# A two-layer decoder on one core: sums of weights formed in the landing buffers, four of these, halved splits of the sums, and a cross output projection with both feature tiles in one bank

## The chip, the core and the metric

The kernel runs on one core of a Trainium2 chip. The metric is the device time of one execution in microseconds (us); lower is better. All inputs and the output lie in device memory; nothing is computed on the host. The engines are TensorE (PE, with its weight load PEld), VectorE (DVE), ScalarE (ACT), GpSimd (POOL) and SyncE (SP), which issues the loads of the weights.

## The reference

Two layers, each of three parts, on 256 tokens of width 2048, all in float32:

```python
for l in range(DEPTH):                                   # DEPTH = 2
    h = rms_norm(x, attn_norm[l])
    (mq, mk, mv, dq, dk, dv, sq, sk, sv, iq, ik, iw) = _split_columns(h @ w_in[l])
    # three kinds of heads: MoBA (6), differential (4), sparse by an index (6)
    mixed = jnp.concatenate([o_moba, o_diff, o_dsa], axis=-1)
    x = x + mixed @ w_out[l]

    h = rms_norm(x, cross_norm[l]); m = rms_norm(mem, mem_norm[l])
    # 4 heads of attention over 256 memory tokens, giving co (256 x 512)
    x = x + co @ cross_wo[l]

    h = rms_norm(x, ffn_norm[l])
    u = h @ ffn_w_up[l]                                  # 2048 -> 2 x 5504
    # a causal convolution over 3 tokens gives uc; g, val = the halves of uc
    x = x + (jax.nn.silu(g) * val) @ ffn_w_down[l]       # 5504 -> 2048
```

The query and key gains of the three kinds of heads (`moba_qk_gain`, `diff_qk_gain`, `dsa_qk_gain`) and the convolution's weights are given per layer.

## The kernel before

**Products in two parts.** Each float32 operand is split in a rounded part `hi` and a rest `lo`, and a product is the sum of two or three matmuls of the parts. Weights are loaded by SP into a landing tile `raw` (8 KB in each partition, three buffers, `RAWS`). `halves` (line 79 on ACT, line 81 on DVE) makes `hi` as a copy of `raw` and then `lo` as `raw` minus `hi`; both tiles have three buffers (`HIS`). A `raw` tile is free again after its `lo`, a `hi` and a `lo` tile after the last matmul that reads them. Activations are split in the same way: `parts` (lines 266 and 267) makes the two tiles `a`.

**Stages of a layer.** The input projection and the three kinds of attention, the output projection with its residual, cross attention with its output projection, the up projection with convolution and gate (21 steps of two tiles and a last one), and the down projection. Tiles of `k`, `t` and `a` are slots of 512 floats in pools that rotate. `mm_rows` (lines 220 to 222) holds the tokens on the output's rows, `up_acc` (lines 242 to 246) the features; there, a pair of 128 features takes two PSUM banks (`mm`, four of them), and a group of weights is 8 blocks of 128 rows.

**Side work.** Everything that isn't a weight stream is written as generators, which a heap runs by a counter of ticks: each group of matmuls calls `tick`, and a generator that yields d goes on d ticks later. `factors` (line 410) yields `G_R`, then sums squares over features by matmuls with ones (line 416), from a tile to which POOL adds one pair after the other (line 408), and makes the root-mean-square factor `rx`. A tile framework then fixes each engine's order of instructions by its own estimate of when operands are ready; so the order on an engine is not that of the code.

**The residual.** `residual` calls `up_acc` for eight pairs of feature tiles, adds them to the residual `xT` and starts `take`, which splits the new `xT` for the next stage. For the cross output projection (`whole=True`) each pair ends with two adds of 256 columns on DVE (line 437), one for each bank.

**The down projection.** `down` runs once for each of two column halves of 1024, over 22 steps: 21 pairs of 128-row blocks of weights and one single block. Seven of the pairs (`SEVEN`) multiply a 2 x 2 block form by the scheme with seven products, the others by eight. The seven-product steps need sums of the activations (`s4`, lines 298 to 301) and of the weights (`tt`, lines 303 to 305, DVE, into a tile `sum` with one buffer), and then two pairs of `hi` and `lo`: one of 3 x 512 columns from `raw`, one of 4 x 512 from `sum`:

```python
tt = wp.tile([P, 4, CH], F32, tag="sum", name="sum", bufs=1)
...
w = halves(b[:, 1:4, :], 3, CH)
sx = parts(s, 4 * P)
wt = halves(tt, 4, CH)
```

Such a step loads its weights with three DMAs (lines 292 to 294), an ordinary one with one (line 318). After the 22 steps `combine` reads eight banks (the four `mm` and four of `at`) with DVE adds and, in the last layer, stores the result (line 1064).

## Time and profile before

| | |
|---|---|
| median of 3 runs | 2567.83 us (2561.11 to 2570.95) |
| the profiled execution's own time | 2556.22 us |
| its span in the profile | 2554.4 us |
| mean granted clock of TensorE | 0.997 |
| PE busy | 2514.4 us, 98% |
| DVE busy | 1910.2 us, 75% |
| ACT busy | 1364.4 us, 53% |
| POOL busy | 162.8 us, 6% |
| moved by DMA | 459.89 MB, mean 180 GB/s |

Busy times are sums over an engine's instructions in one profiled execution. The ends of pipelined matmuls are modelled, so PE's share says little by itself; what tells is where PE stands idle, and for whom. In a row of the waits, the first name is what waited, the one behind the arrow what ended the wait, then come the microseconds, the number of waits and the longest. In a row of the windows come the window, its length, and each engine's busy time with its instructions, the granted clock of TensorE, the DMA engines' busy share and the GB/s.

### The profile page before, as it was taken

To read this page: it belongs to the slowest core of one execution; us is meant where nothing else is said; L and a number is where in the kernel's file an instruction comes from. 1 tells how busy PE (TensorE), PEld (TensorE's weight loads), DVE (VectorE), ACT (ScalarE), POOL (GpSimd) and SP (SyncE) were. 2 spreads that over 40 slices of the span, in tenths; PEclk is the share of its full clock that TensorE was granted. 3 is DMA by queue.
4 is the path that set the end of the run, shared out by engine and by line. 5 is a ranking of instruction groups with operands and counts; after the bars stand their busy time and mean duration, and the time that the engine had idled before them with its cause. 6 is when DMAs were issued, how large, how long until landed. Compare 5 with 4: busy or idle time off the path is not lost. (4 is left out here: it accounts for less than half of the span.)

```text
span 2554.4 us, 34687 instructions
## 1 busy us (share of the span) xinstructions
PE 2514.4 (98%) x13402; PEld 2146.4 (84%) x13402; DVE 1910.2 (75%) x2982; ACT 1364.4 (53%) x1756; POOL 162.8 (6%) x177
## 2 busy tenths in 40 slices
PE   8999999999999999999999999999999999999999
PEld 7778888888888888877787788888888888888777
DVE  6876766677777777889968767666777777778888
ACT  5555565455554555556545555554555555555554
POOL 2210101010000000000041011010100000000000
PEclk9999999999999999999999999999999999999999
DMA  7545546555566656555654555564556665664554
GB/s 240 165 151 177 167 153 201 166 168 189 183 197 186 193 188 192 173 198 173 215 162 146 164 170 164 161 213 133 185 186 193 188 192 184 196 189 163 192 195 152
DMA packets 377705, 459.89 MB, mean 180 GB/s; under 512 B 10638, under 2 KB 331076, under 8 KB 377540
## 3 DMA queue, kind: packets, MB, share of 16 engines
q1 hardware_dynamic: 377540, 457.67, 55.8%
q8 instruction: 105, 1.72, 0.3%
q14 instruction: 60, 0.49, 0.1%
HBM read 455.54 MB, written 2.10 MB: 179 GB/s over the span
## 5 line engine op out<-in xcount | busy, mean ns | idle before, releaser
L81 DVE TENSOR_TENSOR lo<-raw,hi 128x2048 fp32r<-128x2048 f32 (+4 forms) x466 | 969.7, 2084 | 356.0 <-ACT hi L79 354.7
L245 PE MATMUL mm<-k,hi 128*128 128x512 f32 x3136 | 1098.4, 393 | 3.2 <-DVE xT L437 3.2
L79 ACT ACTIVATE hi<-raw 128x2048 fp32r<-128x2048 f32 (+4 forms) x466 | 811.2, 1744 | 434.5 <-PE mm L221 164.0
L246 PE MATMUL mm<-k,lo 128*128 128x256 f32 x3264 | 914.4, 280 | 0.1
L245 PEld LDWEIGHTS mm<-k,hi 128*128 128x128 f32 x3136 | 586.8, 187 | 133.2 <-issue 3.5
L246 PEld LDWEIGHTS mm<-k,lo 128*128 128x128 f32 x3264 | 617.1, 189 | 0.8 <-DVE lo L81 0.5
L220 PE MATMUL mm<-hi,k 128*128 128x512 f32 (+2 forms) x1088 | 413.8, 380 | 0.0
L221 PE MATMUL mm<-hi,k 128*128 128x512 f32 (+2 forms) x1088 | 404.3, 372 | 0.0
L222 PE MATMUL mm<-lo,k 128*128 128x512 f32 (+2 forms) x1088 | 401.6, 370 | 1.0 <-DVE lo L81 1.0
L220 PEld LDWEIGHTS mm<-hi,k 128*128 128x128 f32 x1088 | 206.3, 190 | 35.8 <-issue 3.3
L222 PEld LDWEIGHTS mm<-lo,k 128*128 128x128 f32 x1088 | 205.5, 189 | 36.1 <-DVE lo L81 1.8
L221 PEld LDWEIGHTS mm<-hi,k 128*128 128x128 f32 x1088 | 206.3, 190 | 32.6 <-issue 2.6
L285 PE MATMUL mm<-lo,a 128*128 128x512 f32 x548 | 216.4, 395 | 15.7 <-DVE lo L81 15.7
L283 PE MATMUL mm<-hi,a 128*128 128x512 f32 x548 | 214.6, 392 | 0.2 <-DVE t L1027 0.2
L284 PE MATMUL mm<-hi,a 128*128 128x512 f32 x548 | 214.4, 391 | 0.0
L1040 ACT ACTIVATE t<-t 128x256 f32<-128x256 f32 x86 | 35.7, 418 | 229.3 <-DVE t L1032 229.3
L285 PEld LDWEIGHTS mm<-lo,a 128*128 128x128 f32 x548 | 103.5, 189 | 43.2 <-DVE lo L81 21.9
L1027 DVE TENSOR_TENSOR t<-mm,t 128x256 f32<-128x256 f32 x172 | 68.8, 421 | 90.3 <-ACT t L1024 90.3
L1024 ACT ACTIVATE t<-mm 128x256 f32<-128x256 f32 x172 | 60.2, 375 | 142.2 <-PE mm L246 142.2
L408 POOL TENSOR_TENSOR k<-k,t 128x512 f32<-128x512 f32 x35 | 52.2, 1492 | 1138.0 <-ACT t L407 976.1
L283 PEld LDWEIGHTS mm<-hi,a 128*128 128x128 f32 x548 | 103.7, 189 | 21.6 <-issue 0.6
L284 PEld LDWEIGHTS mm<-hi,a 128*128 128x128 f32 x548 | 103.6, 189 | 21.8
(242 smaller groups left out, 2571.7 us busy)
## 6 DMA issues: line engine op xcount, KB each, us to landing
raw<-in_ffn_w_up_dram SPq DMA_DIRECT2D x168, 1024.0 KB, 5.1
raw<-in_w_in_dram SPq DMA_DIRECT2D x152, 512.0 KB, 4.5
raw<-in_ffn_w_down_dram SPq DMA_DIRECT2D x56, 1024.0 KB, 5.6
raw<-in_w_in_dram SPq DMA_DIRECT2D x20, 1024.0 KB, 5.0
raw<-in_w_out_dram SPq DMA_DIRECT2D x16, 1024.0 KB, 5.5
raw<-in_cross_wkv_dram SPq DMA_DIRECT2D x16, 1024.0 KB, 5.0
raw<-in_ffn_w_down_dram SPq DMA_DIRECT2D x32, 512.0 KB, 5.2
raw<-in_ffn_w_down_dram SPq DMA_DIRECT2D x56, 256.0 KB, 3.8
```

The lines of the kernel that those rows point to most:

```text
L79: nc.scalar.activation(hi, src, AF.Copy)
L81: nc.vector.tensor_tensor(lo, src, hi.bitcast(F32), OP.subtract)
L220: nc.tensor.matmul(o, lhsT=xh, rhs=hi[:, j, :], start=first, stop=False)
L221: nc.tensor.matmul(o, lhsT=xl, rhs=hi[:, j, :], start=False, stop=False)
L222: ins = nc.tensor.matmul(o, lhsT=xh, rhs=lo[:, j, :], start=False, stop=last)
L245: nc.tensor.matmul(outs[i], lhsT=wh, rhs=acts[k], start=first, stop=False)
L246: ins = nc.tensor.matmul(outs[i][:, :S], lhsT=wl, rhs=acts[k][:, :S], start=False, stop=last)
L283: nc.tensor.matmul(bank[q], lhsT=x[0], rhs=w[0], start=first, stop=False)
L284: nc.tensor.matmul(bank[q], lhsT=x[1], rhs=w[0], start=False, stop=False)
L285: return nc.tensor.matmul(bank[q], lhsT=x[0], rhs=w[1], start=False, stop=left[q] == 0)
L1024: nc.scalar.activation(uv[:, S:], outs[i][:, S:], AF.Copy)
L1027: nc.vector.tensor_tensor(u, outs[i][:, :S], v, OP.add)
```

## The change

Six things are changed together.

- Landing buffers `raw` and `hi` buffers go from three to four; `lo` buffers are counted by themselves (`LOS`, three). The tile `sum` is gone, `tmp` has seven buffers and not eight, and the convolution's weights of both layers share one tile.
- In a seven-product step the sums of weights are formed in the landing tile itself, by four adds of 512 columns (line 310 after the change), and these stand behind the step's own `lo`, since they overwrite what it reads.
- `hi` and `lo` of the sums are made in two halves: blocks 0 and 3, then 1 and 2.
- `factors` waits five ticks, or three where it has more to do behind it (in the cross output projection), instead of three.
- In the cross output projection both feature tiles of a pair lie in the halves of one bank, and one add of 512 columns takes them.
- The head gains come per layer, in slots, with three small loads for each layer; in layer 1 these stand between the two groups of index weights.

```diff
@@ -29,9 +29,9 @@
 NEG = -1.0e30
 GONE = -3.0e38
 TOPK = 64
-G_R, G_T, G_S, G_PT, G_DN = 3, 5, 1, 3, 3
+G_R, G_T, G_S, G_PT, G_DN = 5, 5, 1, 3, 3
 FIRST_COL = 3328
-KP, AP, RAWS, HIS = 38, 8, 3, 3
+KP, AP, RAWS, HIS, LOS = 38, 8, 4, 4, 3
 SEVEN = frozenset((2, 5, 8, 11, 14, 16, 18))
 GW = 2 * CH
 
@@ -62,7 +62,7 @@
         return kp.tile([P, CH], F32R, tag="a", name="a", bufs=AP)
 
     def tmp():
-        return tp.tile([P, CH], F32, tag="t", name="t", bufs=8)
+        return tp.tile([P, CH], F32, tag="t", name="t", bufs=7)
 
     def pmm():
         return ps.tile([P, CH], F32, tag="mm", name="mm")
@@ -73,12 +73,14 @@
     def new_raw(a, n):
         return wp.tile([P, a, n], F32, tag="raw", name="raw", bufs=RAWS)
 
-    def halves(src, a, n):
+    def halves(src, a, n, steps=(slice(None),)):
 
         hi = wp.tile([P, a, n], F32R, tag="hi", name="hi", bufs=HIS)
-        nc.scalar.activation(hi, src, AF.Copy)
-        lo = wp.tile([P, a, n], F32R, tag="lo", name="lo", bufs=HIS)
-        nc.vector.tensor_tensor(lo, src, hi.bitcast(F32), OP.subtract)
+        lo = wp.tile([P, a, n], F32R, tag="lo", name="lo", bufs=LOS)
+        for v in steps:
+            nc.scalar.activation(hi[:, v, :], src[:, v, :], AF.Copy)
+        for v in steps:
+            nc.vector.tensor_tensor(lo[:, v, :], src[:, v, :], hi[:, v, :].bitcast(F32), OP.subtract)
         return hi, lo
 
 
@@ -126,8 +128,9 @@
     def attn_g(l):
         return gA[:, l * KT:(l + 1) * KT]
 
+    cw = cst.tile([P, 4, 2 * NF], F32, name="cw")
+
     def load_conv(l):
-        cw = cst.tile([P, 4, 2 * NF], F32, name=f"cw{l}")
         cv = slot()[:2 * NF, :].rearrange("f (j p) -> f j p", p=P)
         nc.sync.dma_start(cv[:, 0:3, :], ffn_conv_w[l].rearrange("j (f p) -> f j p", p=P))
         nc.sync.dma_start(cv[:, 3, :], ffn_conv_b[l].rearrange("(f p) -> f p", p=P))
@@ -140,7 +143,6 @@
             nc.vector.tensor_copy(cw.rearrange("p j f -> p (j f)"), pt[:, :8 * NF])
 
         step(rest())
-        return cw
 
 
 
@@ -228,7 +230,9 @@
     def up_acc(wview, runs, acts, order=None, whole=False):
 
 
-        outs = [pmm() for _ in range(2)]
+
+        outs = [pmm() for _ in range(1 if whole else 2)]
+        own = [outs[0][:, i * S:(i + 1) * S] if whole else outs[i][:, :S] for i in range(2)]
         order = order or EIGHTS
         first = True
         for gi, grp in enumerate(order):
@@ -239,12 +243,12 @@
                 for i in range(2):
                     wh, wl = hi[:, j, i * P:(i + 1) * P], lo[:, j, i * P:(i + 1) * P]
                     if whole:
-                        nc.tensor.matmul(outs[i][:, :S], lhsT=wh, rhs=acts[k][:, :S], start=first, stop=False)
-                        nc.tensor.matmul(outs[i][:, :S], lhsT=wh, rhs=acts[k][:, S:], start=False, stop=False)
+                        nc.tensor.matmul(own[i], lhsT=wh, rhs=acts[k][:, :S], start=first and i == 0, stop=False)
+                        nc.tensor.matmul(own[i], lhsT=wh, rhs=acts[k][:, S:], start=False, stop=False)
                     else:
                         nc.tensor.matmul(outs[i], lhsT=wh, rhs=acts[k], start=first, stop=False)
-                    ins = nc.tensor.matmul(outs[i][:, :S], lhsT=wl, rhs=acts[k][:, :S], start=False,
-                                           stop=last)
+                    ins = nc.tensor.matmul(own[i], lhsT=wl, rhs=acts[k][:, :S], start=False,
+                                           stop=last and (i == 1 or not whole))
                 first = False
                 if j % 4 == 3 or j == n - 1:
                     tick(ins)
@@ -299,18 +303,16 @@
                                         OP.subtract)
                 nc.vector.tensor_tensor(s4[:, 2, :], s4[:, 1, :], a4[:, 0, :], OP.add)
                 nc.vector.tensor_tensor(s4[:, 3, :], a4[:, 2, :], s4[:, 2, :], OP.subtract)
-                tt = wp.tile([P, 4, CH], F32, tag="sum", name="sum", bufs=1)
-                nc.vector.tensor_tensor(tt[:, 0:2, :], b[:, 1::2, :], b[:, 0:1, :].to_broadcast([P, 2, CH]), OP.add)
-                nc.vector.tensor_tensor(tt[:, 2, :], tt[:, 1, :], b[:, 1, :], OP.add)
-                nc.vector.tensor_tensor(tt[:, 3, :], tt[:, 2, :], b[:, 2, :], OP.add)
                 a = parts(act[i], 4 * P)
                 w = halves(b[:, 1:4, :], 3, CH)
                 sx = parts(s, 4 * P)
-                wt = halves(tt, 4, CH)
+                for o, x, y in ((3, 0, 3), (0, 0, 1), (1, 3, 1), (2, 1, 2)):
+                    nc.vector.tensor_tensor(b[:, o, :], b[:, x, :], b[:, y, :], OP.add)
+                wt = halves(b, 4, CH, (slice(0, 4, 3), slice(1, 3)))
                 A, Sx = (lambda j, v=v: [u[:, j * P:(j + 1) * P] for u in v] for v in (a, sx))
                 B, T = (lambda j, v=v: [u[:, j, :] for u in v] for v in (w, wt))
-                todo = {1: (A(0), B(0)), 2: (A(2), B(1)), 3: (Sx(3), B(2)), 4: (A(3), T(3)), 5: (Sx(1), T(0)),
-                        6: (Sx(2), T(2)), 7: (Sx(0), T(1))}
+                todo = {1: (A(0), B(0)), 2: (A(2), B(1)), 3: (Sx(3), B(2)), 4: (A(3), T(2)), 5: (Sx(1), T(0)),
+                        6: (Sx(2), T(1)), 7: (Sx(0), T(3))}
                 for q in (1, 2, 3, 5, 7, 6, 4):
                     ins = product(q, *todo[q])
             else:
@@ -409,7 +411,7 @@
 
     def factors(acc, rest=None):
 
-        yield G_R
+        yield G_R if rest is None else G_R - 2
         pt = pat()
         for t in range(NT):
             for j in range(2):
@@ -432,9 +434,7 @@
             outs = up_acc(wview, [(2 * i * P, 2 * P)], acts, order[i], whole)
             pair = xT[:, 2 * i:2 * i + 2, :].rearrange("p k s -> p (k s)")
             if whole:
-                for j in range(2):
-                    v = xT[:, 2 * i + j, :]
-                    nc.vector.tensor_tensor(v, outs[j][:, :S], v, OP.add)
+                nc.vector.tensor_tensor(pair, outs[0], pair, OP.add)
             else:
                 u = tmp()
                 for j in range(2):
@@ -508,12 +508,19 @@
         nc.gpsimd.tensor_copy(ropeI[:, 1, :, 0, 32:], s)
 
     TAB_W = {"d": 64, "s": 128, "m": 128}
-    head_gain = {}
-    for kind, g in (("d", diff_qk_gain), ("s", dsa_qk_gain), ("m", moba_qk_gain)):
-        gb = cst.tile([P, L, 2, TAB_W[kind]], F32, name="gb" + kind)
-        nc.sync.dma_start(gb.rearrange("p l a d -> p (l a d)"),
-                          g.rearrange("l a d -> (l a d)").unsqueeze(0).to_broadcast([P, L * 2 * TAB_W[kind]]))
-        head_gain[kind] = gb
+    def head_gains(l):
+
+        res, row = {}, None
+        for kind, g in (("d", diff_qk_gain), ("s", dsa_qk_gain), ("m", moba_qk_gain)):
+            n = 2 * TAB_W[kind]
+            if row is None or kind == "m":
+                row, o = slot(), 0
+            nc.sync.dma_start(row[:, o:o + n], g[l].rearrange("a d -> (a d)").unsqueeze(0).to_broadcast([P, n]))
+            res[kind] = row[:, o:o + n].rearrange("p (a d) -> p a d", a=2)
+            o += n
+        return res
+
+    head_gain = head_gains(0)
     lam = slot()
     nc.sync.dma_start(lam, diff_lambda.rearrange("l a d -> (l a d)").unsqueeze(0).to_broadcast([P, L * 256]))
     nlams = cst.tile([P, L], F32, name="nlams")
@@ -533,7 +540,7 @@
 
         w = TAB_W[kind]
         st, h = 128 // w, w // 2
-        gb = head_gain[kind][:, l]
+        gb = head_gain[kind]
         tb = [slot()[:, :NT * 2 * w].rearrange("p (t a d) -> p t a d", t=NT, a=2) for _ in range(2)]
         for a in range(2):
             g1 = gb[:, a, :h].unsqueeze(1).to_broadcast([P, NT, h])
@@ -842,6 +849,8 @@
                 rotary()
                 rope_index()
                 lambdas()
+        if l:
+            head_gain.update(head_gains(l))
         for k in "dsm":
             tabs[k] = rope_table(l, k)
         ib = mm_rows(hT, wv, [(6144 + half, half)], QUADS)
@@ -1009,7 +1018,7 @@
 
         residual(coT, cwo, [[range(2), range(2, 4)]] + [[range(4)]] * 7, gB[:, (2 * L + l) * KT:(2 * L + l + 1) * KT], h3, spread, whole=True)
 
-        cw = load_conv(l)
+        load_conv(l)
 
 
         up = ffn_w_up[l].rearrange("(k p) n -> p k n", p=P)
```

The program's order on three engines, before and after. On DVE in the down projection of layer 1, up to the third seven-product step; before (`lo<-sum` is the rest of a step's sums, `lo<-raw` of 2048 columns that of an ordinary step and of 1536 that of a seven-product step, `a` the rest of activations, lines 303 to 305 the sums of weights):

```order
L81 TENSOR_TENSOR lo<-sum,hi 128x2048
L267 TENSOR_TENSOR a<-k,a 128x512
L303 TENSOR_TENSOR sum<-raw 128x1024
L304 TENSOR_TENSOR sum<-sum,raw 128x512
L81 TENSOR_TENSOR lo<-raw,hi 128x2048
L267 TENSOR_TENSOR a<-k,a 128x512
L81 TENSOR_TENSOR lo<-raw,hi 128x2048
L305 TENSOR_TENSOR sum<-sum,raw 128x512
L267 TENSOR_TENSOR a<-k,a 128x512
L81 TENSOR_TENSOR lo<-raw,hi 128x1536
L267 TENSOR_TENSOR a<-t,a 128x512
```

After (line 83 is the old line 81, 271 the old 267, 304 and 305 the old 300 and 301, and line 310 the sums):

```order
L83 TENSOR_TENSOR lo<-raw,hi 128x2048
L271 TENSOR_TENSOR a<-k,a 128x512
L83 TENSOR_TENSOR lo<-raw,hi 128x2048
L271 TENSOR_TENSOR a<-k,a 128x512
L83 TENSOR_TENSOR lo<-raw,hi 128x1536
L271 TENSOR_TENSOR a<-t,a 128x512
L310 TENSOR_TENSOR raw<-raw 128x512
L304 TENSOR_TENSOR t<-t,k 128x128
L310 TENSOR_TENSOR raw<-raw 128x512
L305 TENSOR_TENSOR t<-k,t 128x128
L310 TENSOR_TENSOR raw<-raw 128x512 x2
L83 TENSOR_TENSOR lo<-raw,hi 128x2x512
```

The sums of a step stood ahead of the `lo` of the ordinary step before it; now they stand behind the 1536 columns of their own step, and the first half of their `lo` (128x2x512) behind them.

On ACT at the same place after the change (line 81 makes `hi`, 270 the rounded activations; the form 128x2x512 is the first half of the sums, the 1024 columns three rows below it, behind the 2048 of the next ordinary step, are the second half):

```order
L81 ACTIVATE hi<-raw 128x2048
L81 ACTIVATE hi<-raw 128x1536
L270 ACTIVATE a<-k 128x512
L270 ACTIVATE a<-t 128x512
L81 ACTIVATE hi<-raw 128x2x512
L270 ACTIVATE a<-k 128x512
L81 ACTIVATE hi<-raw 128x2048
L81 ACTIVATE hi<-raw 128x1024
```

Before, the `hi` of the sums was one instruction of 2048 columns; now there are two, and an ordinary step's `hi` stands between them.

On SP where layer 1 goes from the first column half to the second (the stores of the first half's result and the loads of the second half's first steps); before:

```order
L318 DMA raw<-in_ffn_w_down_dram 128x2x1024
L1064 DMA out_dram<-k 128x512 x2
L292 DMA raw<-in_ffn_w_down_dram 128x512
L1064 DMA out_dram<-k 128x512 x2
L293 DMA raw<-in_ffn_w_down_dram 128x512
L294 DMA raw<-in_ffn_w_down_dram 128x1024
L318 DMA raw<-in_ffn_w_down_dram 128x2x1024 x2
```

After:

```order
L320 DMA raw<-in_ffn_w_down_dram 128x2x1024
L296 DMA raw<-in_ffn_w_down_dram 128x512
L297 DMA raw<-in_ffn_w_down_dram 128x512
L298 DMA raw<-in_ffn_w_down_dram 128x1024
L1073 DMA out_dram<-k 128x512 x2
L320 DMA raw<-in_ffn_w_down_dram 128x2x1024
L1073 DMA out_dram<-k 128x512 x2
L320 DMA raw<-in_ffn_w_down_dram 128x2x1024
```

The three loads of the seven-product step (292 to 294, now 296 to 298) stood between and behind the stores; now they stand ahead of them, and the loads of the ordinary steps between them.

## The prediction

> **What bounds the kernel now.** I read the page first, then the stages by windows, then what TensorE (PE) waits for, then the worst wait instruction by instruction. The page and the windows:
>
> ```profile
> PE 2514.4 (98%) x13402; PEld 2146.4 (84%) x13402; DVE 1910.2 (75%) x2982; ACT 1364.4 (53%) x1756; POOL 162.8 (6%) x177
> ...
> core 0: us, PE busy (x) PEld busy (x) DVE busy (x) ACT busy (x) POOL busy (x), PEclk, DMA share, GB/s
> 1035.00:1286.00 251.00, 243.06 (x1081) 199.63 (x1081) 228.75 (x249) 147.10 (x146) 7.99 (x6) 0.99 0.54 187
> 2310.00:2554.00 244.00, 230.90 (x1008) 187.68 (x1006) 207.87 (x223) 131.49 (x124) 0.00 (x0) 0.99 0.52 176
> 560.00:1035.00 475.00, 474.50 (x2743) 418.28 (x2744) 349.37 (x488) 246.27 (x306) 3.11 (x2) 1.00 0.61 191
> ```
>
> PE is busy in all but 40 us of 2554.4. In the up projection (the last row; the other layer's reads alike) it idles 0.5 us of 475: nothing to win there. The down projections (first two window rows) lose 7.9 and 13.1 us. So the matmuls set the time, and the change can only take back PE's waits:
>
> ```profile
> PE mm L285 <- DVE lo L81: 15.7, 14, 3.5
> PE at L416 <- POOL k L408: 4.9, 3, 2.2
> PE mm L245 <- DVE xT L437: 3.2, 2, 1.6
> PE mm L242 <- DVE xT L437: 2.1, 4, 0.5
> PE at L285 <- DVE lo L81: 1.6, 1, 1.6
> ```
>
> The first and last are the down projections' 15 waits for a `lo` tile; L416 is the sum of squares behind POOL's adds; the L437 rows are the cross output projection waiting for a PSUM bank. The longest wait of the last layer, on PE and then on DVE:
>
> ```profile
> 2376.23 0.39 PE L283 MATMUL mm<-hi,a 128*128 128x512 f32 x1
> 2376.46 0.39 PE L284 MATMUL mm<-hi,a 128*128 128x512 f32 x1
> 2379.32 0.50 PE L285 MATMUL mm<-lo,a 128*128 128x512 f32 x1 [2.48 <-DVE lo L81]
> ...
> 2380.59 0.63 PE L283 MATMUL mm<-hi,a 128*128 128x512 f32 x1
> ```
>
> ```profile
> 2371.76 0.69 DVE L267 TENSOR_TENSOR a<-k,a 128x512 fp32r<-128x512 f32 x1
> 2375.11 1.23 DVE L303 TENSOR_TENSOR sum<-raw 128x1024 f32<-128x1024 f32 x1 [2.66 <-DMA raw<-in_ffn_w_down_dram]
> 2376.37 0.69 DVE L304 TENSOR_TENSOR sum<-sum,raw 128x512 f32<-128x512 f32 x1
> 2376.98 2.28 DVE L81 TENSOR_TENSOR lo<-raw,hi 128x2048 fp32r<-128x2048 f32 x1
> ```
>
> PE lacks the `lo` that DVE starts at 2376.98. DVE stood until 2375.11 at the sums of a *later* seven-product step, whose load had not landed, and did two of them first. An ordinary step is 0.23 us (2376.23 to 2376.46); this one took 2.86, so a wait costs 0.15 us more than the idle time shown. The `lo` falls short because of a queue order and a late load, not because DVE lacks time: DVE idles 22.3 us of the first window and 36.1 of the second.
>
> **The change part by part.**
>
> *Sums in place, four landing buffers, hi and lo buffers counted apart.* The sums now stand behind the `lo` of their own step (the two DVE pieces shown with the change), so none waits for a load ahead of another step's `lo`. Loads start earlier: a fourth buffer, and the three loads of a seven-product step that stood behind the output stores now stand ahead of them. The related waits:
>
> ```profile
> DVE sum L303 <- DMA raw<-in_ffn_w_down_dram: 14.9, 8, 2.7
> DVE lo L81 <- ACT hi L79: 11.4, 8, 2.5
> ACT hi L79 <- PE mm L284: 60.3, 15, 7.9
> ```
>
> (all from the window 2310 to 2554). The last two are the chain of three `hi` buffers: PE frees one, ACT fills it in 1.91 us, only then comes DVE's `lo`, 2.29 (rows below). With four, `hi` is ready before its `lo` buffer is free, and 1.91 us leave that chain. At stake is 15.7 + 1.6 = 17.3 us of idle, 15 x 0.15 = 2.3 hidden, and the slow clock behind the longest wait:
>
> ```profile
> 2376.40:2385.00 8.60, 6.12 (x20) 4.52 (x20) 8.60 (x8) 1.81 (x2) 0.00 (x0) 0.80 0.55 180
> 1286.00:1296.00 10.00, 7.80 (x31) 6.09 (x31) 9.62 (x17) 3.16 (x3) 9.69 (x15) 0.83 0.42 120
> 1727.00:1737.00 10.00, 8.63 (x36) 6.80 (x35) 7.52 (x18) 2.06 (x2) 1.98 (x1) 0.83 0.35 118
> ```
>
> A granted clock of 0.80 over 8.6 us costs 1.7 us; the PE rows above show it too, 0.63 a matmul instead of 0.39. Together 21.3 us. I take three quarters, 16 us: what stays is at the change of column half, where the combining operations fill DVE in both kernels. The ends are 7 (a third) and 21.3.
> The Trainium skill ("TensorE: Matmul & The Clock Gate", Part 1) says that the clock falls to half only after an idle window of about 3.4 us. By that rule the gaps here, all under 3 us, would not cause the slow stretches, and the sum would win back 3.4 us less (this 1.7 and the 1.7 taken in the next part); the rows show half speed within 1.3 us of a 2.86 us step, so the sum goes by them.
>
> *What it adds on DVE and ACT.* Mean durations in the last window:
>
> ```profile
> L81 DVE TENSOR_TENSOR lo<-raw,hi 128x2048 fp32r<-128x2048 f32 x26 | 59.5, 2287 | 5.7 <-ACT hi L79 5.7
> L303 DVE TENSOR_TENSOR sum<-raw 128x1024 f32<-128x1024 f32 x13 | 15.9, 1224 | 19.1 <-DMA raw<-in_ffn_w_down_dram 14.9 <-issue 3.6 <-DVE t L298 0.6
> L81 DVE TENSOR_TENSOR lo<-raw,hi 128x1024 fp32r<-128x1024 f32 x2 | 2.4, 1220 | 0.0
> L79 ACT ACTIVATE hi<-raw 128x2048 fp32r<-128x2048 f32 x26 | 49.7, 1912 | 42.0 <-PE mm L284 22.4 <-issue 19.6
> L79 ACT ACTIVATE hi<-raw 128x1024 fp32r<-128x1024 f32 x2 | 2.1, 1055 | 3.2 <-PE mm L284 3.2
> ```
>
> Per seven-product step the sums go from 1.22 + 2 x 0.69 (the L304 row above) = 2.60 to 4 x 0.69 = 2.76 us, the `lo` of the sums from 2.29 to 2 x 1.22 = 2.44: 0.31 us, over 28 steps 8.7 us on DVE. The idle 22.3 + 36.1 us hides it; without that cover it is 8.7 on the path.
> The Trainium skill ("VectorE: DVE Perf Modes", Rules for kernel authors) advises to minimize the count of DVE operations, which speaks against two more per step; were DVE the bound, the sum would be 8.7 us worse, and the rows say it is not.
> The new wait is larger. The `hi` of the second half stands on ACT behind the next step's whole `hi` (1.91), in some steps behind an `a` too. Between the two `lo` halves DVE has 1.22 us of the first half and perhaps 0.69 of an `a`, ACT has 1.91 + 1.06 to do: DVE can stand 1 to 1.5 us per step, with the next plain `lo` queued behind it on DVE and PE behind that. 28 x 1.5 = 42 us of DVE time against 58 us idle: mostly covered. I take 2 us on the path (ends 0 and 42 - 17 = 25, if DVE can use only the 17 us in which PE waits today).
>
> *The sum of squares two ticks later (not in the cross output projection).* A tick here is 12 matmuls, 2.8 us at 0.23, so L416 moves 5.5 us back; the longest wait is 2.2, so all three end. They cost 4.9 + 3 x 0.15 = 5.4 us and are followed by two stretches at 0.83, 10 x 0.17 = 1.7 each. I take 5.4 and half of the 3.4: 7.1 us (ends 5.4 and 8.8). The scale factor is first used after eight ticks, so nobody waits.
>
> *Cross output projection in one bank.* A pair of feature tiles holds one PSUM bank, not two, so PE may run four pairs ahead. It then waits for DVE's weights:
>
> ```profile
> 551.68 1.21 DVE L81 TENSOR_TENSOR lo<-raw,hi 128x1024 fp32r<-128x1024 f32 x1
> 552.81 1.91 DVE L186 SCALAR_TENSOR_TENSOR k<-xT,gains,k 128x256 fp32r<-128x256 f32 x2
> 554.65 0.74 DVE L437 TENSOR_TENSOR xT<-mm,xT 128x256 f32<-128x256 f32 x2
> 555.31 2.27 DVE L81 TENSOR_TENSOR lo<-raw,hi 128x2048 fp32r<-128x2048 f32 x1
> ...
> 559.89 0.47 PE L245 MATMUL mm<-k,hi 128*128 128x512 f32 x1 [1.58 <-DVE xT L437]
> ```
>
> DVE needs 3.63 us per pair (551.68 to 555.31), one add of 0.69 for two that take 0.74 hardly changes that. But PE's first up matmul, at 559.89, would no longer wait for the seventh pair's add, only for the `lo` that ends at 557.6: 2.3 us earlier in each layer. I take 4.6 us of the 3.2 + 2.1 + 6 x 0.15 = 6.2 (ends 2 and 6.2).
>
> *Head gains per layer, one conv tile, seven scratch tiles.* In layer 1 three small loads stand in SP's queue between the index weights, and POOL's tables wait for them. POOL makes the tables early and uses them late:
>
> ```profile
> 1289.22 0.50 POOL L541 TENSOR_TENSOR k<-cosT,gbd 128x64 f32<-128x64 f32 x1
> 1355.82 0.73 POOL L557 TENSOR_TENSOR t<-k 128x256 f32<-128x256 f32 x1 [16.35 <-ACT k L567]
> ```
>
> 66 us of cover; if it went, POOL's 9.69 us of the 1286 row above would show. SP's wait for a free slot has the fourth landing buffer as cover. Taken at 0, ends 0 and 3. The up projection keeps its rate: its evacuations come one `lo` (2.29 us) later on DVE, and a PSUM pair is needed again only one group (16 x 2 x (0.23 + 0.12) = 11 us) later.
>
> *Sum.* -16 + 2 - 7.1 - 4.6 = -25.7 us. The profiled execution took 2556.2 us: 2530.5. The median of the runs, 2567.83, is 1.0045 times that: 2542.
>
> **The rivals.**
> *A: the down projections gain nothing,* since the wait for the second half's `hi` replaces the wait for loads. For it: ACT's order. Against: DVE's 58 us idle. The other parts, 11.7 us, remain: 2544.5, as a median 2556.
> *B: slower; ACT's order makes DVE the bound there.* Its place is the second half's `hi` in all 28 steps; its price 1.5 + 0.31 us each, 51 us. It decides once DVE can't move its idle time under these waits: past about 1 us per step on the path (28 us) it eats all gains. With 1.5 us per step on the path (42 us) beside what the loads give back nothing, the sum is 42 - 11.7 = +30: 2586, as a median 2598. For it: the first window's DVE is busy in 228.75 of 251 us, and 14 steps x 0.31 bring that to 233. Against it: the `lo` buffers let DVE work one step ahead, 5 us.
> *C: the loads are the bound.* The windows show 176 to 187 GB/s and a DMA share of 0.52 to 0.54 in the down projections, the up projection 191 at 0.61 without a wait; so there is room. If a fourth buffer only queues behind the same engines, a third of the 21.3 us comes back: -7 + 2 - 11.7 = -16.7, 2539.5, as a median 2551.
>
> **How the numbers follow.** Forecast 0.65, C 0.10, A 0.12, B 0.13. Forecast ends: best -21.3 - 8.8 - 6.2 = -36.3, a median of 2531; worst, all terms at their small ends and 3 us added, -7 + 2 - 5.4 - 2 + 3 = -9.4, a median of 2558. The range 2530 to 2560 takes these in with A and C. About 0.5% (12.8 us, a median of 2555) is what a measurement of this kernel can tell from no change. Faster by more: most of the forecast (0.61) and C (0.10), 0.71; within: the forecast's weak end 0.04 and A 0.12, 0.16; slower: B, 0.13.
>
> **What would show it.** Right: the 15 PE waits for `lo` fall below 6 us in sum; no DVE sum waits for a load; the L416 and L437 waits vanish; PE idles under 22 us in all, and the up windows stay at 475. Wrong: DVE waits for ACT's `hi` grow past 30 us in the down projections and PE's waits with them (A or B); ACT or DVE still waits for loads there (C); or a wait appears in the up projection or the index stage, which I priced at nothing.

## The result, and the profile after

The changed kernel takes 2535.47 us in the median (2534.38 to 2536.75, 4 runs) against 2567.25 us before (2561.11 to 2570.95): a ratio of 0.9879, 95% interval 0.9858 to 0.9899. That is 31.8 us faster; 25.7 were forecast, and the median lies 6.5 us below the forecast, inside the range. The profiled execution took 2534.38 us, only 21.8 less than the profiled one of before. The two numbers differ for a reason that the prediction did not have, so the stages come first. Each is read from the trace, from its first matmul to the first of the next (the last one to the end of the span); "again" is a second profiled execution of the same program.

| stage, us | before | before again | after | after again |
|---|---|---|---|---|
| input projection and heads, layers 0 and 1 | 343.1, 344.4 | 342.9, 344.3 | 342.0, 340.9 | 343.0, 340.9 |
| output projection | 97.4, 97.1 | 96.4, 97.1 | 95.8, 95.8 | 95.8, 95.8 |
| cross attention | 80.0, 81.6 | 80.0, 81.6 | 78.7, 78.7 | 78.7, 78.7 |
| cross output projection | 28.6, 28.6 | 28.6, 28.6 | 25.0, 25.0 | 25.0, 25.0 |
| up projection | 479.6, 481.2 | 479.6, 481.2 | 483.8, **495.5** | 483.9, 485.4 |
| down projection | 237.6, 244.6 | 234.6, 244.0 | 229.6, 230.9 | 229.5, 230.9 |
| span | 2554.4 | 2550.0 | 2532.6 | 2523.6 |

The page and PE's waits after the change:

```profile
PE 2513.5 (99%) x13402; PEld 2146.4 (85%) x13402; DVE 1918.0 (76%) x3022; ACT 1383.5 (55%) x1784; POOL 168.4 (7%) x177
```

```profile
PE at L376 <- DMA k<-in_x_dram: 3.8, 5, 2.0
PE at L142 <- DMA k<-in_ffn_conv_w_dram: 3.7, 2, 1.9
PE at L121 <- DMA k<-in_attn_norm_dram: 2.5, 1, 2.5
PE at L142 <- DMA k<-in_ffn_conv_b_dram: 1.2, 2, 0.7
PE at L618 <- DVE mx L620: 0.9, 2, 0.5
PE mm L224 <- DVE lo L83: 0.8, 1, 0.8
PE at L418 <- POOL k L410: 0.8, 2, 0.4
PE at L287 <- ACT hi L81: 0.6, 1, 0.6
PE at L289 <- DVE lo L83: 0.5, 1, 0.5
```

The 17.3 us of waits for a `lo` in the down projections are 0.5, the 4.9 at the sum of squares 0.8, and the cross output projection's 5.3 are gone. New are the L142 rows: PE waits 4.9 us for the convolution's weights at the head of the up projections. The windows by stage (down, down, up, up):

```profile
1036.00:1266.00 230.00, 228.75 (x1011) 187.26 (x1010) 219.21 (x261) 142.18 (x147) 3.99 (x3) 1.00 0.55 194
2301.00:2532.00 231.00, 227.66 (x1015) 187.90 (x1013) 212.02 (x256) 134.19 (x137) 0.00 (x0) 1.00 0.52 180
553.00:1036.00 483.00, 480.05 (x2766) 423.58 (x2765) 351.08 (x490) 252.09 (x306) 3.48 (x2) 1.00 0.61 190
1807.00:2301.00 494.00, 491.32 (x2775) 426.47 (x2774) 351.45 (x491) 254.03 (x308) 3.47 (x2) 0.99 0.60 187
```

The last two rows are the same work. PE is idle for 2.95 and 2.68 us in them, and yet one is 11 us longer. Two stretches of 20 us inside these stages, in the first profile after and then in the second:

```profile
906.00:926.00 20.00, 20.00 (x118) 17.65 (x117) 13.75 (x22) 9.88 (x13) 0.00 (x0) 1.00 0.61 182
1906.00:1926.00 20.00, 20.00 (x115) 17.41 (x114) 14.48 (x22) 9.74 (x13) 0.00 (x0) 1.00 0.53 162
```

```profile
906.00:926.00 20.00, 20.00 (x117) 17.51 (x116) 14.56 (x22) 9.79 (x13) 0.00 (x0) 1.00 0.56 172
1906.00:1926.00 20.00, 20.00 (x118) 17.62 (x117) 13.74 (x20) 10.31 (x13) 0.00 (x0) 1.00 0.65 195
```

No wait, a granted clock of 1.00, and 115 matmuls in one stretch where the others have 117 or 118. From start to start in the trace, a pair of matmuls (512 and 256 columns) takes 346.7 ns at the faster pace (steps of 347, 346, 347) and 353.3 at the slower (349, 350, 361, and again). Behind its first 24 pairs each up projection here keeps its pace to its end: 1376 pairs x 6.6 ns = 9.1 us. The two executions after the change differ by 9.0 us in span; this stage differs by 10.1, the first input projection by 1.0 the other way. With no slow up projection on either side (first profile before, second after) the change is worth 2554.4 - 2523.6 = 30.8 us. The output projections are not of equal pace in these two: most of their pairs ran at 353.3 ns before and at 346.7 after, and nearly all of the 2.9 us by which these two stages are shorter is this.

### The profile page after: what moved, and what is told of

Its sections match the earlier page's. It is cut to its first block, busy times and chain, and to the rows that moved or that the text cites. A ratio compares the mean times of both kernels' runs of the same rounds, so it can differ in the third digit from the quotient of the medians.

```text
span 2532.6 us, 34711 instructions
## 1 busy us (share of the span) xinstructions
PE 2513.5 (99%) x13402; PEld 2146.4 (85%) x13402; DVE 1918.0 (76%) x3022; ACT 1383.5 (55%) x1784; POOL 168.4 (7%) x177
## 4 chain that ended last, share of the span: by engine, by line
PE 95%; DVE 3%; DMA 1%; ACT 0%; issue 0%; SPq 0%; DVEq 0%; ACTq 0%
PE mm L249 30%; PE mm L250 16%; PE mm L222 9%; PE mm L223 9%; PE mm L224 9%; PE mm L289 5%; PE mm L287 5%; PE mm L288 5%; PE at L618 1%; DVE lo L83 1%; PE at L289 1%; PE at L287 1%; PE at L288 1%; PE at L593 1%; DMA k<-in_ffn_conv_b_dram 1%; DVE k L188 1%
## 5 line engine op out<-in xcount | busy, mean ns | idle before, releaser
L83 DVE TENSOR_TENSOR lo<-raw,hi 128x2048 fp32r<-128x2048 f32 (+3 forms) x522 | 1047.6, 2012 | 427.3 <-ACT t L1033 215.2
L249 PE MATMUL mm<-k,hi 128*128 128x512 f32 x3136 | 1109.5, 397 | 0.0
L81 ACT ACTIVATE hi<-raw 128x2048 fp32r<-128x2048 f32 (+3 forms) x522 | 866.1, 1670 | 367.2 <-PE mm L223 178.9
L1038 ACT ACTIVATE t<-t,cw 128x256 f32<-128x256 f32 x172 | 94.2, 595 | 117.7 <-DVE t L1037 117.7
L1039 DVE SCALAR_TENSOR_TENSOR t<-t,cw 128x255 f32<-128x255 f32 x172 | 82.6, 481 | 33.5 <-ACT t L1038 33.5
```

Source lines behind the costliest of these rows:

```text
L81: nc.scalar.activation(hi[:, v, :], src[:, v, :], AF.Copy)
L83: nc.vector.tensor_tensor(lo[:, v, :], src[:, v, :], hi[:, v, :].bitcast(F32), OP.subtract)
L249: nc.tensor.matmul(outs[i], lhsT=wh, rhs=acts[k], start=first, stop=False)
L1038: nc.scalar.activation(v, u, AF.Identity, scale=cw[:, 2, f:f + 1], bias=cw[:, 3, f:f + 1])
L1039: nc.vector.scalar_tensor_tensor(v[:, 1:], u[:, :S - 1], cw[:, 1, f:f + 1], v[:, 1:], op0=OP.mult, op1=OP.add)
```

## The experiments

Times are medians of a study's own runs. Where a profile has up projections at the slower pace, 9 us each come off before it is compared.

**Three landing buffers.**

```diff
-KP, AP, RAWS, HIS, LOS = 38, 8, 4, 4, 3
+KP, AP, RAWS, HIS, LOS = 38, 8, 3, 4, 3
```

> The changed kernel with three landing buffers instead of four, all else kept. The down projections took 229.6 and 232.3 us in the changed kernel and 237.6 and 246.1 before; PE waited 17.3 us for lo tiles before and 0.5 after. Theory 1 (the gain there is the place of the sums, behind their own step's lo, so that no load stands ahead of another step's lo on DVE): PE's waits for lo stay under 5 us and the whole time rises by at most 5 us over the changed kernel. Rival (the gain is the earlier load that the fourth buffer gives; the sums in place even hold a buffer longer, so three are worse than before): PE's waits for lo return to 12 us or more and the whole time rises by 12 to 25 us.

2571.61 us (2569.63 to 2574.72), slower than before beside it (ratio 1.0072, 1.0057 to 1.0087). Both up projections ran at the slower pace; the span of 2572.9 less 18 is 2555, that of before. The down projections took 239.5 and 247.9 us. The waits of PE, DVE and ACT in the second:

```profile
PE at L289 <- DVE lo L83: 10.1, 8, 1.8
```

```profile
DVE lo L83 <- ACT hi L81: 30.5, 20, 3.7
```

```profile
ACT hi L81 <- DMA raw<-in_ffn_w_down_dram: 43.0, 12, 6.9
```

DVE no longer waits for a load; it waits 30.5 us for ACT's `hi`, and ACT waits 43.0 for the load (10.1 before). The load is still late; another engine meets it first. PE's waits for `lo` over the whole program are 14.9 us. Theory 1 falls: with three landing buffers the sums behind their own step's `lo` bring nothing. At equal pace the rise over the second profile after is about 31 us, more than the rival's 12 to 25. (The 232.3 and 246.1 us of the expectation are 230.9 and 244.6 in the table above.)

**The sums in a tile of their own, four landing buffers.** The four in-place adds give way to the old three into `sum` and one whole split; three `hi` buffers.

```diff
-                wt = halves(b, 4, CH, (slice(0, 4, 3), slice(1, 3)))
+                wt = halves(tt, 4, CH)
```

> The changed kernel with the sums of weights as before, in a tile of their own with one buffer and one whole split, with four landing buffers kept and three hi buffers (there is no room for four). Theory 1 (the place of the sums on DVE): the sums again stand ahead of other steps' lo, so PE's waits for lo return to 8 us or more and the time rises by 8 to 20 us. Rival (the earlier load): with four landing buffers the loads are there when the sums want them, PE's waits for lo stay under 5 us and the time within 4 us of the changed kernel.

2528.47 us (2528.28 to 2529.1), ratio 0.9903 (0.9887 to 0.9920); both up projections at the faster pace, down projections 229.5 and 230.4 us, as in the changed kernel. Of DVE's waits in the second:

```profile
DVE lo L83 <- ACT hi L81: 16.6, 11, 2.2
...
DVE sum L307 <- DMA raw<-in_ffn_w_down_dram: 0.4, 1, 0.4
```

The sums wait 0.4 us for loads instead of 14.9. The rival holds: the fourth landing buffer is the gain of the down projections; of the edits that touch this stage, the run keeps only that one and the seven scratch tiles. The sums in place neither make it nor are needed for it.

**The in-place sums split whole.**

```diff
-                wt = halves(b, 4, CH, (slice(0, 4, 3), slice(1, 3)))
+                wt = halves(b, 4, CH)
```

> The changed kernel with hi and lo of the sums whole, not in halves. In the prediction the split costs DVE 0.15 us a step and lets the second half's hi wait behind another step's hi on ACT: priced at 2 us on the path. If that is so, the whole form is 1 to 4 us faster. Rival (the split is what lets DVE and PE begin early on the sums, 1 us sooner in each of 28 steps): the whole form is 3 to 15 us slower, with PE waits for lo or hi in the seven-product steps.

2555.12 us (2544.32 to 2563.66), the time of before (ratio 1.000, 0.998 to 1.002), with both up projections of the profile at the slower pace. The down projections took 241.5 and 238.1 us. PE's waits in the first:

```profile
PE at L287 <- ACT hi L81: 7.6, 4, 3.1
PE mm L289 <- DVE lo L83: 1.6, 1, 1.6
```

19 us come from the halves, more than even the rival's 15: PE now waits for the sums' `hi`. By the code, that `hi` can start in place only when all four adds are done; in halves it starts after two. The prediction had them as a cost.

**Three hi buffers.**

```diff
-KP, AP, RAWS, HIS, LOS = 38, 8, 4, 4, 3
+KP, AP, RAWS, HIS, LOS = 38, 8, 4, 3, 3
```

> The changed kernel with three hi buffers instead of four. The prediction said that a fourth takes ACT's 1.91 us out of the chain from PE's freeing a buffer to DVE's lo. If that chain was a part of the gain: DVE's waits for ACT's hi in the down projections rise by 5 us or more over the changed kernel's and the whole time by 2 to 8 us. Rival (hi was never late enough to matter, since the lo buffers, still three, limit DVE first): the time stays within 2 us.

2530.75 us (2530.73 to 2531.44), both up projections at the faster pace. Down projections 231.8 and 231.6 us, 2.9 more than after; DVE's waits for `hi` there are 8.8 + 9.5 us, against 3.2 + 4.9. The span, 2528.9, is 5.3 over the second profile after. The rest lies mostly in the up projections (485.5 and 486.9 us), where PE waits 3.6 us for POOL's add, against 0.8 after. The fourth `hi` buffer has its part, a small one.

**The sum of squares after three ticks.**

```diff
-G_R, G_T, G_S, G_PT, G_DN = 5, 5, 1, 3, 3
+G_R, G_T, G_S, G_PT, G_DN = 3, 5, 1, 3, 3
...
-        yield G_R if rest is None else G_R - 2
+        yield G_R
```

> The changed kernel with the sum of squares after three ticks everywhere, as before. Priced in the prediction at 5.4 to 8.8 us, by three waits of PE for POOL's add (4.9 us) and the slow clock behind two of them: the time rises by 5 to 9 us, with the waits back at the sum of squares and a lowered clock behind them. Rival (these waits had another cause, for instance DVE held by the sums of the down projection, and are gone without the ticks): within 2 us.

2543.35 us (2532.13 to 2551.05). Its span of 2539.4, with the same up projections as the first profile after, is 6.8 longer, and that is one place: the input projection of layer 1 took 347.5 us instead of 340.9. PE's wait there and 14 us around it, then the same 14 us of the changed kernel:

```profile
PE at L418 <- POOL k L410: 3.4, 1, 3.4
```

```profile
1276.00:1290.00 14.00, 10.55 (x39) 8.79 (x39) 7.34 (x17) 2.60 (x3) 2.94 (x1) 0.76 0.22 61
```

```profile
1276.00:1290.00 14.00, 14.00 (x67) 11.70 (x66) 8.68 (x18) 3.83 (x5) 2.98 (x1) 1.00 0.45 130
```

The cross attention stages take 78.7 us each, as in the changed kernel; their two waits of before didn't come back.

**The cross output projection in two banks, in the changed kernel; and in one bank, alone, in the kernel before.** The first puts the old lines back, the second makes the new ones the only edit. Of the first, one line:

```diff
-        outs = [pmm() for _ in range(1 if whole else 2)]
+        outs = [pmm() for _ in range(2)]
```

> The changed kernel with the cross output projection in two banks and two adds as before. Theory (one bank took the waits for the bank away, and the time was given back at the convolution's loads): the cross output stages go from 24.9 and 25.0 us back to 28.6, the L142 waits of 4.9 us shrink or vanish, and the whole time stays within 4 us. Rival (one bank is a plain gain): the whole time rises by 5 to 8 us.

> The kernel before with one part of the change alone: both feature tiles of the cross output projection in one bank and one add. The changed kernel with two banks kept 25.7 us in those stages against 28.6 before, so the bank is not needed there. If the bank alone is also enough: the two stages take 25 us instead of 28.6, the convolution's loads are then waited for, and the time falls by 0 to 6 us. Rival (the gain of these stages came from the landing and hi buffers alone): they stay above 27 us and the time within 2 us of before.

Two banks: 2538.72 us (2534.37 to 2542.46); span 2532.6 with one slow up projection, as after. The two stages took 25.7 us, not 28.6, and L142 waited 5.0 us. So with the new buffers the bank is worth 0.7 us a stage. One bank alone: 2567.62 us (2557.44 to 2576.25), no faster than before beside it (ratio 1.0024, 1.0000 to 1.0047). Its two stages did fall to 25.0, and the up projection behind the first rose from 479.6 to 485.3. The convolution's loads are waited for there too (3.1 us), for the first time in the kernel before:

```profile
PE at L139 <- DMA k<-in_ffn_conv_w_dram: 2.4, 2, 1.3
...
PE at L139 <- DMA k<-in_ffn_conv_b_dram: 0.7, 2, 0.4
```

More is lost to POOL's add for the sum of squares, which is waited for at the heads of both up projections too: 8.7 us in five waits, against 4.9 in three before.

```profile
PE at L417 <- POOL k L409: 8.7, 5, 2.2
```

Either the bank or the new buffers free this stage, and what they free is given back at the next.

**The convolution's loads earlier.**

```diff
+        conv = load_conv(l)
         residual(coT, cwo, ...
-        load_conv(l)
+        step(conv)
```

> The changed kernel with the two loads of the convolution's weights issued ahead of the cross output projection's weights instead of behind the first up loads. In the changed kernel PE waits for them in both layers (3.7 + 1.2 us idle at L142, none before the change), and the clock falls behind it. Theory (the cross output projection's gain is given back there): the L142 waits vanish, the stretch from the cross output projection to the down projection shortens by 3 to 6 us in each layer, and the time falls by 5 to 12 us. Rival (the load is only what shows; the R broadcast, the sum of squares or the lo of the up weights is late next): the wait moves to another line and the time falls by under 2 us.

2529.51 us (2528.78 to 2537.68). The changed kernel's PE at that place, which this edit is to mend:

```profile
560.91 0.28 PE L250 MATMUL mm<-k,lo 128*128 128x256 f32 x1
561.58 1.05 PE L418 MATMUL at<-ones,k 128*128 128x1 f32 x8 [0.39 <-POOL k L410]
564.52 0.44 PE L142 MATMUL at<-ident,k 86*128 86x86 f32 x3 [1.89 <-DMA k<-in_ffn_conv_w_dram]
565.63 0.41 PE L142 MATMUL at<-ident,k 86*128 86x86 f32 x1 [0.67 <-DMA k<-in_ffn_conv_b_dram]
565.76 0.77 PE L249 MATMUL mm<-k,hi 128*128 128x512 f32 x1
```

The L142 waits are gone, and a part of them is late next, the broadcast of the scale factor:

```profile
PE at L1016 <- DVE t L1015: 3.1, 2, 1.5
```

At the faster pace the up projection of layer 1 took 483.0 instead of 485.4 us; that of layer 0 was at the slower here, 490.3, less 9 is 481.3 instead of 483.9. Some 2.5 us each, so 5 in all: just below the 3 to 6 expected of each stage; the rival, that the wait moves on, is right for the rest. The median, 1.2 us under that of the changed kernel beside it (2530.7), doesn't show them: the paces, 9 us a stage, lie over it.

**The changed kernel again.**

> The changed kernel once more. In its profile the up projection of layer 1 ran at 353.3 ns for a pair of matmuls (512 and 256 columns) throughout, that of layer 0 at 346.7, with no wait in between; before the change both ran at 346.7 and the output projections at 353.3. If the pace is drawn at each restart of PE, by chance, the two stages show another combination here in one case of two, and the time differs from 2534.4 by 0 or 9 us a stage (1344 pairs x 6.6 ns). Rival (it is fixed by the program): layer 0 at 346.7 and layer 1 at 353.3 again.

2530.7 us (2525.42 to 2536.83). Layer 1 at the faster pace this time: the pace isn't fixed by the program. The two programs with three `hi` and four landing buffers stayed within 0.8 us over four runs each; so it seems that how free the draw is differs from one program to another.

**A break in the alternation.**

```diff
+                if first and not whole:
+                    nc.tensor.matmul(outs[0][:, :P], lhsT=zero, rhs=acts[k][:, :P], start=False, stop=False)
```

> The changed kernel with the early convolution loads, and with one more matmul of 128 columns (by a matrix of zeros, so that it adds nothing) behind the first two pairs of each of the 43 groups of the up projection and the 8 of the output projection. If the pace of 346.7 or 353.3 ns for a pair is set anew by each break in the alternation of 512 and 256 columns: the pace changes within the stages, so that neither up projection is wholly at one of them. Rival (only a real stop of PE sets it): each up projection keeps one pace from its start to its end. The extra matmuls cost 86 x 0.06 = 5 us and some more.

2550.69 us (2550.05 to 2551.66, 10 runs). The up projections took 494.5 and 496.0 us, nearly all of it at the slower pace, but not all. In layer 1 the pairs from 1839.9 to 1849.9 us start 350 and 343 ns apart in turn, the faster pace. Then comes an extra matmul, and behind it the steps are 349, 350, 361 to the end:

```profile
1849.90 0.40 PE L251 MATMUL mm<-k,hi 128*128 128x512 f32 x1
1850.14 0.28 PE L252 MATMUL mm<-k,lo 128*128 128x256 f32 x1
1850.26 0.22 PE L255 MATMUL mm<-k,zero 128*128 128x128 f32 x1
1850.32 0.45 PE L251 MATMUL mm<-k,hi 128*128 128x512 f32 x1
```

PE does not stop there, so the rival falls: a break in the alternation is enough to change the pace. Why the slower one follows nearly every one of these breaks stays open.

**Another order of the matmuls.** On top of the early loads, the lines for `wl` stand in a loop of their own, so that a row block runs 512, 512, 256, 256:

```diff
+                for i in range(2):
+                    wl = lo[:, j, i * P:(i + 1) * P]
                     ins = nc.tensor.matmul(own[i], lhsT=wl, ...
```

> The changed kernel with the early convolution loads, and in the up and output projections the matmuls of a row block in the order 512, 512, 256, 256 columns instead of 512, 256, 512, 256. If the two paces belong to the alternation, both vanish: the stages take one length, the same in both layers, and the down projections stay at 229.5 and 231 us. A pace of 340 ns or less for a pair would make the whole 15 us or more faster, one above 353 slower by as much. Rival (the paces don't depend on the order): 346.7 or 353.3 again.

2524.43 us (2524.04 to 2525.02), ratio 0.9872 (0.9849 to 0.9894). The up projections took 483.5 and 485.2 us, the 1.7 us between the layers being there at the faster pace before as well (479.6 and 481.2). Behind their heads both run at 348.3 ns for a pair throughout, and the runs lie within 1.0 us of each other:

```profile
906.00:926.00 20.00, 20.00 (x116) 17.44 (x115) 13.63 (x21) 9.83 (x12) 0.00 (x0) 1.00 0.59 186
1906.00:1926.00 20.00, 20.00 (x117) 17.47 (x116) 14.07 (x19) 10.12 (x12) 0.00 (x0) 1.00 0.58 181
```

Both stretches lie between the two paces, near the faster. This kernel is below every one of the eight timed runs of the changed kernel (2525.42 to 2536.83), but not timed in one study with it, and the ratios to the kernel before beside each overlap (0.9851 to 0.9918 for the changed one): that it is faster is not shown. Nor do four close runs show by themselves that the draw is gone, since two programs with the old order were as close.

**The kernel before again.**

> The kernel before once more, for a second look at its paces. Its profiled execution took 2556.2 us with both up projections at the faster pace, its other runs 2561 to 2571. If the pace explains this, an execution of 2560 us or more shows one or both up projections at 353.3 ns, about 9 us each, and the rest of the stages as in the first profile within 2 us. Rival (the difference lies in the waits for loads): both at 346.7 and the down projections longer.

2551.75 us, both up projections at the faster pace, so the case that was to tell did not come up. What differs from the first profile is the down projection of layer 0 (234.6 against 237.6) and the output projection of layer 0 (96.4 against 97.4). The latter shows the pace changing within a stage. In both executions its pairs go from 353.3 to 346.7 ns behind side matmuls at 365 us, and back to 353.3 behind the next ones at 372. Near 394.5 two matmuls of 512 columns once stand side by side; from there the first execution stays at 353.3 to the end, and the second goes on at 346.7. The same break in the same program was followed by either pace.

## Why the prediction was right, point by point

- **What bounds the kernel**: right. PE idles 19.1 us in the profile after, 40.0 before; the forecast was under 22.
- **The down projections, -16, and +2 for the split**: -21.8 measured, just past the far end of 21.3, because nothing stayed at the change of column half (PE shows no wait in the second down projection and 1.1 us in the first). Half of the mechanism was wrong. The text put the stall down to a queue order and a late load; the load alone decides, as three landing buffers and the sum tile with four show. The +2 had the wrong sign: against the whole form the halves bring 19 us, and DVE's waits for `hi` fell from 20.4 us (9.0 + 11.4) to 8.1 instead of growing past 30. After the change they are, in the first and the second down projection:

```profile
DVE lo L83 <- ACT hi L81: 3.2, 5, 1.1
...
DVE lo L83 <- ACT hi L81: 4.9, 7, 1.2
```

- **The sum of squares, -7.1**: the stages where the three waits stood became 7.8 us shorter (the input projection of layer 1 by 3.5, cross attention by 1.3 and 2.9), so the size is right. But only one of the three is the ticks' doing: in the changed kernel they are worth 6.8 us, all in the input projection. The two waits in cross attention were gone with three ticks as well, and no run shows which edit took them away. That the sum came out is in part luck.
- **The cross output projection, -4.6**: this step failed. The stages gained 7.2 us, over the 6.2 given as the most, and the up projections behind them lost 4.3 + 4.2 = 8.5, so the sum is +1.3. Missing was what is late next: 3.6 us earlier, PE meets the loads of the convolution's weights, issued at 556.22 us in the trace and landed when PE goes on at 564.5. The prediction followed PE to the `lo` that ends at 557.6 and no further, and priced the convolution's part at nothing; a wait in the up projection was its own sign of being wrong.
- **The slow clock**: the stretches at half the clock behind the waits of before are gone, and one at the head of each up projection is new. As in the profile before, it falls behind short stops. After 561.58 PE did only the short matmuls above, with 0.39, 1.89 and 0.67 us idle, and the next of 512 columns took 0.77. From 565.2 the granted clock is 0.50 for 3.4 us, which costs 1.7; with the 2.6 us of waits at L142 that is the 4.3 us that this stage lost. With the early loads the mean clock of the whole execution is 1.000. By the Trainium skill ("TensorE: Matmul & The Clock Gate", Part 1) the clock falls to half after an idle window of about 3.4 us. No single gap here is that long, and shorter ones were enough elsewhere: 2.48 us idle in the prediction's rows, and in the run with three `hi` buffers 1.56 us (behind one of 0.29), among matmuls of 512 columns alone:

```profile
1163.45 0.40 PE L288 MATMUL mm<-hi,a 128*128 128x512 f32 x1
1165.41 0.50 PE L289 MATMUL mm<-lo,a 128*128 128x512 f32 x1 [1.56 <-DVE lo L83]
1165.74 0.58 PE L287 MATMUL mm<-hi,a 128*128 128x512 f32 x1
1166.12 0.63 PE L288 MATMUL mm<-hi,a 128*128 128x512 f32 x1
```

The prediction's "all under 3 us" overlooks its own row with a longest wait of 3.5: that one, in the first down projection, has a slow stretch behind it too (from 1168.3 us), which the sum left out.
- **The sum and the median**: -25.7 forecast, -30.8 between the two profiles with fast up projections. That these are close is partly luck: the down projections gave 7.8 more than -16 + 2, the cross output projection 5.9 less than forecast, and 2.9 came from the output projections' pace, for which the forecast had no term and of which no run shows the cause. Taking the profiled execution times 1.0045 for the median failed: after the change it is 1.0004. The runs of before lay between 2548.08 and 2573.86 us over all studies, those of the changed kernel between 2525.42 and 2536.83; a profile is one draw of these. Part of this spread is the pace. In the kernel before the up projections' share was not seen, as both profiles were at the faster one; the down projections there also differ from one execution to the next (237.6 and 234.6), and after the change they don't.
- **The rivals**: A (no gain in the down projections) is out at -21.8. B, slower by ACT's order, did not come: DVE's waits for `hi` are 8.1 us, not 1.5 in each of 28 steps. That a wait for ACT's `hi` can take the whole gain is shown by the whole sums, but there without the split that B was about. C was right on what binds, the load, and wrong on what a fourth buffer does about it.

## What to carry to other kernels

Follow a stage that gets faster into the next one: list every load and side task that PE meets there, with the time at which it lands, before the gain is booked. If a wait ends on a late load, reordering the waiting work can just move the wait to another engine, as here; the fourth landing buffer took it away. Compare stage by stage, and count matmuls in a stretch without waits: two profiles of one program can differ by 9 us without a difference in PE's waits.

## What the hardware showed beside

- Matmuls of 512 and 256 columns in alternation run at 346.7 ns a pair (steps of 347, 346, 347, or of 350 and 343) or at 353.3 (349, 350, 361), with a granted clock of 1.00 and no wait, and can keep to it for 480 us; the same program was seen at both. The pace can change, either way, where the alternation is broken: by side matmuls, by one extra matmul of 128 columns, or by two of 512 columns side by side. In the order 512, 512, 256, 256 both up projections ran at 348.3 ns. The runs' spread was 1.0 us there and 8.9 with the early loads alone, but only 0.7 and 0.8 in two programs with the old order. What decides between the paces stays open.
- With three landing buffers the down projections took 234.6 to 248 us, from one execution and program to another; with four, 229.5 to 231.8 in every profile but that of the whole in-place split.
